# Layer 1's modulation, moved from behind layer 0's mixer to the look-ups of layer 0's expert search

## The chip, the cores and the metric

One core of a Trainium2 chip runs the whole kernel in one launch. The metric is the time of the kernel on the device in microseconds (us). Before the change it is 5706.96 us (median of 3 runs, 5706.85 to 5725.06).

## The reference

Two layers run over 512 latent tokens `x` and 256 context tokens `ctx`, 1024 wide. Everything is float32.

```
silu_c, silu_cc = silu(c), silu(c_ctx)
for l in range(2):
    mod_x = split(silu_c  @ w_mod[l] + b_mod[l], 6)      # shift, scale, gate, twice; (1024) @ (1024, 6144)
    mod_c = split(silu_cc @ w_mod[l] + b_mod[l], 6)
    h_c = layer_norm(ctx) * (1 + mod_c[1]) + mod_c[0]
    mix_c, states = token_mixer(h_c)                     # four branches; in the last layer only the states
    ctx = layer_norm(a * ctx + mod_c[2] * mix_c)
    h_c = layer_norm(ctx) * (1 + mod_c[4]) + mod_c[3]
    ctx = layer_norm(a * ctx + mod_c[5] * peer_ffn(h_c)) # not in the last layer
    # the same for x, whose scans start from the context's states
peer_ffn(h): q = h @ wq; two top-16 searches of 128 keys for each of 8 heads, top-16 of their sums,
             act = gelu(h . u[id]) * softmax(score), out = sum over 8 * 16 experts of act * v[id]
```

The modulation needs `c`, `c_ctx`, `w_mod` and `b_mod` alone. It can be made at any time before the layer that uses it.

## The kernel before

**Staging.** A layer 0 runs like this: modulation; the context's projections and scans, with x's gates and branches beside them; the context's expert search (`peer_front`); x's projections and scans (`recurrent`, in the phase "m2") with the context's expert gathers beside them; the branches' ends and the output projection (`mix_out`); x's expert search; then the experts of x. Of x's four token tiles, tile 3 gathers its experts' rows one by one; tiles 0 to 2 run through all 16384 experts densely, in chunks of 128 experts: `dense_u` (24 matmuls a chunk, of a hi and a lo part that ScalarE and VectorE split), `gates_all` (which turns the look-ups' results into gate tiles), and `dense_uv`, `dense_v`.

**The modulation.** `mod_steps(l, groups, fm)` (L466) is a generator. For each of 12 groups of 512 columns it loads 8 tiles of 256 KB through SyncE's queue, multiplies each with the 2 columns of silu(c), silu(c_ctx) into one PSUM row pair, copies the row with ScalarE, transposes it in 4 pieces, and adds the bias on VectorE into `fm` ("modfm"), with one more add for the scales. Then it yields. In float32 the profile shows two records for each of its matmuls.

**Lanes.** A helper's buffers have a prefix. In the lane "x" the weight tiles are "xwraw" and the PSUM tiles "pa" (2 banks); without a prefix they are "wraw" and "ps" (6 banks). For layer 0 there are 5 "xwraw" buffers during the mixer; in the expert search there are 3 "wraw" buffers (`WF`, L47).

**What sets the order.** The program is traced in one order. A planner then puts the instructions of each engine into a fixed order by priorities (the count of the trace), by data that is ready in its own reckoning of time, and by free buffers; each engine and SyncE's DMA queue run that order strictly. Fillers (`add`, `step`, `fill`, `drain`) are generators in lane "x" whose pieces are traced with a priority at least 200 later (`LOW`). `tick` traces pieces of the context's gathers with a priority 3000 later and not before what was traced ahead of them; it gives fixed numbers of pieces to the steps of x's scans (`RT`, `TL`). So an instruction that is traced late runs early where its engine would stand idle and its buffers are free: layer 1's modulation is traced as a filler behind `mix_out` (L1877 to L1879), but needs only silu(c) and free "xwraw" buffers, and the trace has it at 1207 to 1436 us, beside x's scans.

**The expert search.** `peer_front` (L1767) first projects the queries in 8 units (`peer_scores`), for each of which `topk_head` makes the top-16 lists of the four token tiles on VectorE; behind each of these `fill(n)` traces one dense chunk (`FD`). Then comes, for the tiles in the order 3, 0, 1, 2:

```
for i in order:
    top = self.topk(tk[i])          # the look-ups: one-hot products on VectorE
    ...                             # tile 3: gather_in, and rows for its tokens
    self.fill(m)                    # FT = 1 dense chunk
    ...                             # tiles 0 to 2: dense_in, transposes of ids and gates
```

Of the kernel before, what the change touches and what calls it, by code (L numbers as in the profile page):

```python
# [53 lines left out]
FT = 1  # L54
UO = 64
FD = 1
# [128 lines left out]
class K:  # L185
# [1578 lines left out]
                self.nc.sync.dma_start(a, acts[c])  # L1764
                self.v_chunk(l, c, a, w, acc, vv, False, c == N - 1)

    def peer_front(self, l, x, fm, s, h, order, dense=None, n=0, m=0):  # L1767


        NT = len(x)  # L1770

        self.lo_pool = True
        tk = [self.topk_tiles() for _ in range(NT)]

        def fn(u, S):
            for i in order:
                self.topk_head(u, S[i], tk[i])
                self.fill(n)
        self.peer_scores(l, h, NT, fn)
        self.lo_pool = False  # L1780
        gg, late = [], []
        for i in order:
            with self.section() as sec:
                top = self.topk(tk[i])
                if dense is not None and i < ND:

                    late.append((i, top))
                else:
                    gg.append((i, self.gather_in(l, *top)))
            self.fill(m)  # L1790
            while late and (late[0][0] != i or i == order[-1]):
                self.dense_in(*late.pop(0), *dense)
            if gg and (dense is None and len(gg) == NT or dense is not None and len(gg) == 1 and i == gg[0][0]):
                with self.section(sec):
                    rows = [self.bcast_row(fm, g, s, 1.0) for g in (3, 4)]
                    gg = [(i, (self.h_tokens(x[i], rows),) + g) for i, g in gg]
        return [g for _, g in gg]

    def run(self):
        io = self.io  # L1800
        x = [io["x"][i] for i in range(4)]
        c = [io["ctx"][i] for i in range(2)]
        y = [io["y"][i] for i in range(4)]
        fm = None
        for l in range(L):
            last = l == L - 1
            self.nw = {"": WB[l], "x": WX[l]}
            self.extra = {"": WE[0][l], "x": WE[1][l]}
            x1 = [self.d([128, 1024], f"x1_{i}", 2) for i in range(4)]
# [3 lines left out]
            with ExitStack() as mix:  # L1813
                hx = self.hx()

                mx = self.merged(512, hx)
                mix.enter_context(self.phase("mix"))
                mix.enter_context(self.sharing())
                with self.phase("m1", s1=s1, s2=s2, xs2=xs2):
                    hT = self.t([128, 2, 8, 256], "hT", 1, F32R)  # L1820
                    if fm is None:
                        fm = self.mod(0, range(4))
                    hc = self.norm_mod(c, fm, 0, 1, hT)
                    if not last:
                        self.add(self.mod_steps(l, range(4, 12), fm))
                        gates = self.add(self.gates(l, hc, 256, mc[0]))
                        self.add(self.pool_branch(l, hc, 2, 1, mc))
                        self.add(self.four_branch(l, hc, 2, 1, mc))
                    self.add(self.norm_steps(x, fm, 0, 0, hx))
                    hx = self.parts(hx)  # L1830
                    gatesx = self.add(self.gates(l, hx, 512, mx[0], range(4 if last else 2)))
                    self.add(self.pool_branch(l, hx, 4, 0, mx))
                    self.add(self.four_branch(l, hx, 4, 0, mx))
                    if not last:
                        fm1 = self.keep([128, 48, 2], "modfm", 2)
                        gatesy = self.add(self.gates(l, hx, 512, mx[0], range(2, 4)))

                    def branch(b, y, after):
                        self.add(self.scanned(l, b, hc, 2, mc, y, after), after=gates)
                    states = self.recurrent(l, hc, 2, [None] * 4, not last, FC[l], branch)  # L1840
                    states = [self.put_state(st) for st in states]
                    if not last:
                        while len(mc[2]) < 8:
                            self.fill()
                        self.mix_out(l, c, c1, fm, 1, mc[2])
                        hT = self.t([128, 2, 8, 256], "hT", 1, F32R)
                        self.lo_pool = True
                        h = self.norm_mod(c1, fm, 3, 1, hT)
                        gc = self.peer_front(l, c1, fm, 1, h, range(2), None, FC[l][6], FC[l][6])
                        accs = [self.d([128, 1024], "gacc", 4) for _ in range(2)]  # L1850
                        rows = self.gather(l, gc, accs)
                        self.ticking(rows)
                        while len(self.fillers) > 1:
                            self.fill()
                            self.tick(RE)
                    elif self.fillers[:1] != [gatesx]:
                        self.finish()
                with self.phase("m2", **(dict(s2=M2X[0], xs2=M2X[1]) if last else dict(s2=M2, s4=3, xs2=M2Y))):
                    lane = "x" if last else ""

                    def branch(b, y, after):
                        if last or b == 3:
                            self.add(self.scanned(l, b, hx, 4, mx, y, after), lane, gatesx if last else None)
                        else:
                            y = {c: self.put_state(t, "y", 4) for c, t in y.items()}
                            late.append(self.scanned(l, b, hx, 4, mx, y, after))
                    late = []
                    self.tick(RT[0])
                    self.recurrent(l, hx, 4, states, True, FX[l], branch)
                    for g in late:  # L1870
                        self.add(g, lane, gatesx)
                    while self.fillers:
                        self.fill()
                        self.tick(RT[6])
                    self.ticked()
                    hT = self.mix_out(l, x, x1, fm, 0, mx[2], self.hx)
                    if not last:  # L1877
                        self.add(self.mod_steps(l + 1, range(12), fm1))
                        self.drain()  # L1879
            if not last:  # L1880
                at = self.tc.cur_priority
                self.tc.cur_priority += GP
# [6 lines left out]
            it = [self.t((128, ND * 128), f"it{k}", 1, F16) for k in range(2)]  # L1889
            gp = self.t((128, 2, ND * 128), "gp", 1, F16)  # L1890
# [6 lines left out]
            self.extra = {"": 0, "x": 0}  # L1897
            with self.phase("fx", s2=4, s4=2, x4=2):
                self.add(gu)
                gx = self.peer_front(l, x1, fm, 0, hT, (3, 0, 1, 2), (it, gp), FD, FT)  # L1900
                self.fillers.clear()
            gen = self.gather(l, gx, [accx])
            with self.area("wk", side="right") as wk:
# [48 lines left out]
            x = x2  # L1952
            if not last:
                fm = fm1
# [119 lines left out]
```

## Time and profile before

| | us |
|---|---|
| median of the runs | 5706.96 |
| the profiled execution | 5714.13 |
| its span (core 0) | 5712.4 |
| TensorE busy | 4988.2 |
| VectorE busy | 4243.9 |
| ScalarE busy | 1949.3 |
| GpSimd busy | 1614.6 |

PE is TensorE, PEld its weight loads, DVE VectorE, ACT ScalarE, POOL GpSimd, SPq SyncE's DMA queue. Layer 0 takes the first 3300 us or so. All instructions carry line L150, a helper that records each operation; the names of the tiles tell them apart: `pa<-xwraw,sc` is a modulation matmul, `pa<-masks,xs` the transpose of its row, `ps<-hx,whi` a projection, `ps<-s,s` and `ps<-s,masks` scan work, `gat` the gathers, `oh` and `sel` the look-ups, `hx,dh` and `hx,dl` a dense chunk, `acts` its result.

### The profile page before, as it was taken

What the parts mean: (1) busy time and instruction counts of PE and PEld (TensorE: products, weight loads), DVE (VectorE), ACT (ScalarE), POOL (GpSimd) and SP (SyncE); (2) the same over time, 40 slices, a digit from 0 to 9 for tenths busy, and PEclk for the clock granted to TensorE, in tenths of its full rate; (3) what the DMA queues carried; (4) which work ended last, traced back from release to release, by engine and by line L of the source; (5) the groups of instructions that cost most, each with busy time, mean ns of one, the idle gap of its engine ahead of it and who ended that gap; (6) DMA issues with size and microseconds to landing.
All of it is one profiled execution on the core that took longest, in us unless ns stands there. A gap on an engine that the chain in (4) does not pass through costs nothing. (4 is left out here: it accounts for less than half of the span.)

```text
span 5712.4 us, 76827 instructions
## 1 busy us (share of the span) xinstructions
PE 4988.2 (87%) x26902; PEld 4198.0 (73%) x26902; DVE 4243.9 (74%) x8063; ACT 1949.3 (34%) x3711; POOL 1614.6 (28%) x1226
## 2 busy tenths in 40 slices
PE   8998878889457786699999979999888979999997
PEld 3787755763456685699987868787677969999886
DVE  3665777878778889898777786467565579977777
ACT  2444421321003332254333344233134324433333
POOL 0000344333444552444332210000002434443221
PEclk9999998989668898899999989999998989999999
DMA  6555589888878774799889863434434339988897
GB/s 214 176 167 177 166 301 321 275 277 288 276 261 296 258 236 153 256 357 343 299 306 349 317 214 125 134 103 134 129 119 135 126 109 335 363 299 314 320 332 244
DMA packets 618070, 1372.35 MB, mean 240 GB/s; under 512 B 95569, under 2 KB 229329, under 8 KB 614865
## 3 DMA queue, kind: packets, MB, share of 16 engines
q1 hardware_dynamic: 470224, 830.50, 43.0%
q0 software_dynamic: 147456, 536.94, 27.3%
q8 instruction: 211, 3.46, 0.2%
q14 instruction: 179, 1.46, 0.1%
HBM read 1225.64 MB, written 141.56 MB: 239 GB/s over the span
## 5 line engine op out<-in xcount | busy, mean ns | idle before, releaser
L150 POOL DMA_INDIRECT gat<-in_u,gidx x512 | 692.6, 1353 | 964.5 <-DVE gat L150 886.3
L150 POOL DMA_INDIRECT gat<-in_v,gidx x512 | 629.5, 1229 | 1166.3 <-DVE gacc L150 1046.7
L150 PE MATMUL ps<-hx,dh 128*128 128x384 f32 x2944 | 759.8, 339 | 0.9 <-ACT dh L150 0.9
L150 DVE SCALAR_TENSOR_TENSOR gacc<-gat,gact,gacc 128x1024 f32<-128x1024 f32 x508 | 658.7, 1297 | 96.7 <-DMA gat<-in_v,gidx 88.8
L150 DVE SCALAR_TENSOR_TENSOR gat<-gat,hb 128x1024 f32<-128x1024 f32 x512 | 618.0, 1218 | 127.1 <-DMA gat<-in_u,gidx 125.3
L150 PE MATMUL ps<-s,s 128*128 128x128 f32 (+3 forms) x2752 | 421.3, 311 | 160.3 <-issue 84.8
L150 PEld LDWEIGHTS ps<-s,s 128*128 128x128 f32 (+1 forms) x2752 | 376.7, 214 | 231.2 <-issue 119.6
L150 PEld LDWEIGHTS ps<-hx,dh 128*128 128x128 f32 x2944 | 535.4, 190 | 8.4 <-ACT dh L150 2.6
L150 PE MATMUL ps<-hx,dl 128*128 128x384 f32 x1472 | 497.6, 338 | 34.3 <-DVE dl L150 34.3
L150 ACT CAST dh<-du 128x1024 fp32r<-128x1024 f32 x256 | 269.2, 1052 | 754.4 <-PE ps L150 518.9
L150 DVE TENSOR_TENSOR vl<-dv,vh 128x1024 fp32r<-128x1024 f32 x256 | 313.3, 1224 | 200.8 <-ACT vh L150 197.4
L150 ACT CAST xwhi<-xwraw 128x512 fp32r<-128x512 f32 x352 | 217.7, 620 | 518.4 <-PE pa L150 389.7
L150 PE MATMUL ps<-hx,whi 128*128 128x512 f32 x1152 | 381.0, 399 | 8.5 <-ACT whi L150 8.4
L150 ACT CAST vh<-dv 128x1024 fp32r<-128x1024 f32 x256 | 269.2, 1052 | 341.4 <-PE ps L150 237.6
L150 PE MATMUL pa<-hx,xwhi 128*128 128x512 f32 x1152 | 376.3, 404 | 4.8 <-DVE ld L150 2.3
L150 ACT CAST whi<-wraw 128x512 fp32r<-128x512 f32 x320 | 197.9, 621 | 487.6 <-PE ps L150 272.2
L150 DVE TENSOR_TENSOR xwlo<-xwraw,xwhi 128x512 fp32r<-128x512 f32 x352 | 242.8, 692 | 159.8 <-ACT xwhi L150 149.2
L150 PE MATMUL pa<-hx,dh 128*128 128x384 f32 x1152 | 338.3, 358 | 10.5 <-ACT da L150 10.4
L150 PE MATMUL ps<-vl,gh 128*128 128x512 f32 x1024 | 318.2, 392 | 0.0
L150 PE MATMUL ps<-vh,gh 128*128 128x512 f32 x1024 | 317.4, 393 | 0.0
L150 PE MATMUL ps<-vh,gl 128*128 128x512 f32 x1024 | 317.2, 391 | 0.0
L150 PEld LDWEIGHTS ps<-hx,dl 128*128 128x128 f32 x1472 | 279.2, 190 | 36.1 <-DVE dl L150 36.0
(291 smaller groups left out, 10898.3 us busy)
## 6 DMA issues: line engine op xcount, KB each, us to landing
du<-in_ut SPq DMA_DIRECT2D x256, 512.0 KB
dv<-in_v SPq DMA_DIRECT2D x256, 512.0 KB
xwraw<-in_w_in SPq DMA_DIRECT2D x272, 256.0 KB
wraw<-in_w_in SPq DMA_DIRECT2D x176, 256.0 KB
xwraw<-in_w_mod SPq DMA_DIRECT2D x160, 256.0 KB
acts<-da SPq DMA_DIRECT2D x176, 192.0 KB
rest<-wst SPq DMA_DIRECT2D x48, 704.0 KB
W<-rest SPq DMA_DIRECT2D x22, 1536.0 KB
```

The source lines that it names most:

```text
L150: r = f(*a, **kw)
```

## The change

Layer 1's modulation is no longer a filler behind `mix_out`. `peer_front` takes a generator `beside` and advances it three steps (three of 12 column groups) behind each token tile's look-ups, so that four tiles take all 12. It now runs without a prefix: weight tiles "wraw", PSUM "ps", row "s2" of the phase "fx", at the search's own priority and not 200 later. In the last layer `beside` is empty. The context's `peer_front` is called without it.

```diff
-    def peer_front(self, l, x, fm, s, h, order, dense=None, n=0, m=0):
+    def peer_front(self, l, x, fm, s, h, order, dense=None, n=0, m=0, beside=iter(())):
...
                     gg.append((i, self.gather_in(l, *top)))
+            for _ in range(3):
+                next(beside, None)
             self.fill(m)
...
                     hT = self.mix_out(l, x, x1, fm, 0, mx[2], self.hx)
-                    if not last:
-                        self.add(self.mod_steps(l + 1, range(12), fm1))
-                        self.drain()
...
                 self.add(gu)
-                gx = self.peer_front(l, x1, fm, 0, hT, (3, 0, 1, 2), (it, gp), FD, FT)
+
+                beside = iter(()) if last else self.mod_steps(l + 1, range(12), fm1)
+                gx = self.peer_front(l, x1, fm, 0, hT, (3, 0, 1, 2), (it, gp), FD, FT, beside)
+                self.run_all(beside)
                 self.fillers.clear()
```

## Rows read from the trace of the kernel before

**Rows 1.** The page, part 1: busy us, share of the span, instructions.

```profile
PE 4988.2 (87%) x26902; PEld 4198.0 (73%) x26902; DVE 4243.9 (74%) x8063; ACT 1949.3 (34%) x3711; POOL 1614.6 (28%) x1226
```

**Rows 2.** Table of stretches of layer 0: from:to, length, busy us by engine.

```profile
core 0: us, PE busy (x) PEld busy (x) DVE busy (x) ACT busy (x) POOL busy (x), PEclk, DMA share, GB/s
1242.00:1446.00 204.00, 174.13 (x610) 75.67 (x608) 166.53 (x324) 40.57 (x69) 63.94 (x54) 0.93 0.81 278
1446.00:1720.00 274.00, 148.75 (x753) 133.18 (x752) 214.69 (x268) 24.38 (x44) 138.37 (x115) 0.66 0.82 274
1720.00:1990.00 270.00, 197.97 (x1199) 172.43 (x1198) 229.18 (x315) 97.36 (x221) 125.07 (x100) 0.87 0.81 279
1990.00:2180.00 190.00, 156.97 (x768) 139.25 (x767) 161.91 (x667) 52.25 (x92) 99.59 (x74) 0.93 0.68 227
2180.00:2312.00 132.00, 87.98 (x439) 81.22 (x439) 123.39 (x372) 37.16 (x51) 19.25 (x15) 0.83 0.40 131
2312.00:2370.00 58.00, 53.39 (x337) 51.76 (x336) 49.84 (x47) 21.17 (x47) 35.41 (x21) 0.97 0.93 326
2370.00:2430.00 60.00, 28.90 (x172) 27.78 (x170) 39.09 (x49) 10.98 (x32) 27.93 (x19) 0.72 0.81 263
2430.00:3300.00 870.00, 855.64 (x4670) 765.56 (x4669) 709.66 (x869) 349.71 (x644) 304.66 (x228) 0.99 0.92 328
```

**Rows 3.** Groups of instructions, 1242 to 1446: busy us, mean ns | idle before, releaser.

```profile
L150 PE MATMUL pa<-xwraw,sc 128*2 128x512 f32 x178 | 87.0, 612 | 7.1 <-DMA xwraw<-in_w_mod 6.9
...
L150 PE MATMUL ps<-hx,whi 128*128 128x512 f32 x80 | 25.8, 416 | 5.4 <-ACT whi L150 5.4
...
L150 PE MATMUL pa<-masks,xs 2*128 2x2 f32 x48 | 4.9, 202 | 6.2 <-ACT xs L150 6.2
```

**Rows 4.** Time line of TensorE in x's scans: start us, us, instruction.

```profile
1368.63 2.74 PE L150 MATMUL pa<-xwraw,sc 128*2 128x512 f32 x6
1371.30 1.12 PE L150 MATMUL ps<-s,masks 128*128 128x512 f32 x2
...
1375.01 1.02 PE L150 MATMUL pa<-xwraw,sc 128*2 128x512 f32 x2 [0.77 <-DMA xwraw<-in_w_mod]
...
1380.16 1.02 PE L150 MATMUL pa<-xwraw,sc 128*2 128x512 f32 x2 [0.94 <-DMA xwraw<-in_w_mod]
1382.11 1.02 PE L150 MATMUL pa<-xwraw,sc 128*2 128x512 f32 x2 [0.93 <-DMA xwraw<-in_w_mod]
```

**Rows 5.** Stretch table of the gathers' tile alone: DVE, ACT, POOL busy.

```profile
1242.00:1446.00 204.00, 64.28 (x106) 0.00 (x0) 63.94 (x54) 0.93 0.81 278
```

**Rows 6.** Time line of SyncE's queue at the end of the expert scores.

```profile
2159.01 0.33 SPq L150 DMA_DIRECT2D wraw<-in_wq  x1
2166.56 4.49 SPq L150 DMA_DIRECT2D acts<-da  x2
```

**Rows 7.** Tile "wraw", 0 to 70 us: ns min/median/max, first and last start.

```profile
L150 PE MATMUL ps<-wraw,sc x64: 590/592/1057, 9.5 to 64.5; 128*2 128x512 f32 x64
L150 SPq DMA_DIRECT2D wraw<-in_w_mod x32: 327/328/431, 4.2 to 60.4; - x32
```

**Rows 8.** Time line of TensorE: part of a dense chunk, one record left out.

```profile
2249.39 0.51 PE L150 MATMUL pa<-hx,dh 128*128 128x384 f32 x2
...
2249.91 0.51 PE L150 MATMUL pa<-hx,dh 128*128 128x384 f32 x2
```

**Rows 9.** Groups of instructions, 2180 to 2312.

```profile
L150 DVE TENSOR_TENSOR dl<-du,dh 128x1024 fp32r<-128x1024 f32 x15 | 18.3, 1217 | 0.7 <-ACT dh L150 0.7
```

**Rows 10.** Waits from 2370 to 2430: us in total, times, longest.

```profile
PE ps L150 <- DVE dl L150: 25.0, 2, 15.2
```

**Rows 11.** Time line of TensorE in the look-ups, with idle time before.

```profile
2266.51 0.45 PE L150 MATMUL ps<-masks,sel 128*128 128x128 f32 x1 [10.54 <-DVE sel L150]
...
2282.57 0.45 PE L150 MATMUL ps<-masks,sel 128*128 128x128 f32 x1 [4.10 <-DVE sel L150]
...
2290.28 0.69 PE L150 MATMUL pa<-hx,dl 128*128 128x384 f32 x1 [7.26 <-DVE dl L150]
```

## The prediction, made before the change was run

> **What bounds the kernel now.** I read the page first for shares: TensorE 87% of the span, VectorE 74%, so no engine is full over the whole kernel and the stage decides [rows 1]. Then a table of stretches around the two places of the change [rows 2]. In it the reader sees four regimes. From 1242 to 1446 us (x's scans: projections and the four state-space chunks) TensorE is busy 174.1 of 204 us and VectorE 166.5. From 1446 to 1990 both have room. From 2180 to 2312 (end of the expert scores, then the look-ups) VectorE is the bound, 123.4 of 132 us, and TensorE has 44 us free. From 2430 to 3300 TensorE is full, 855.6 of 870 us, so work that is late at 2430 is paid in full afterwards.
>
> Then the groups of the first stretch [rows 3]: 87.0 us of TensorE's 174.1 is the modulation's matmuls (178 of 192 records, two to a loaded tile), 4.9 us its row transposes; TensorE also stands idle 7.1 us for the modulation's loads and 6.2 us for its row copies. The time line [rows 4] shows why that matters: the scan's short matmuls (two of 1.12 us) stand in one in-order queue between modulation pieces of 1 to 2.7 us, and at 1375.01, 1380.16 and 1382.11 the piece at the head waits for a load while scan work stands behind it. So the modulation is no free filler there; it sits on the path that sets the end of the stretch. How much of it comes back depends on VectorE, where 64.3 us are the context's gathers [rows 5].
>
> **The change, part by part.**
>
> *Removed from x's scans.* TensorE loses 87.0 + 4.9 us of work and 7.1 + 6.2 us of waits, 105 us at most [rows 3]; the stretch could then be 99 us on TensorE alone. VectorE doesn't allow that: without the 64.3 us of gathers it has 166.5 - 64.3 = 102 us [rows 2, 5]. The gathers have a far later priority and may slide. If half of them stay, VectorE has 134 us; at 93%, the highest share that it reaches in these stretches short of the full one (123.4/132), that is 143 us, and 204 - 143 = 61 us are won. Bounds: 105 us if only TensorE held the stretch; if all gathers stay, 166.5/0.93 = 178, or 26 us; no loss, for even at 1.2 GHz throughout TensorE's other 82 us would be some 153.
>
> From that goes a clock loss. With the modulation TensorE is busy 85% and its granted clock is 0.93; in the stretch right behind it is busy 54% at 0.66, and at 73% the clock is 0.87 [rows 2]. What remains is 174 - 92 = 82 us; in 143 us that is 57%. I take 0.75: 82 x (0.93/0.75 - 1) = 20 us, half of it on the path, 10 us. Won: 51 us. The Trainium skill says in "TensorE: Matmul & The Clock Gate", section "Part 1: The HAM clock gate", that the array is throttled by default and only activity releases it, 1.2 against 2.4 GHz. The trace agrees (0.66 behind the stretch, 0.93 in it), and it is a rule against this change, since the modulation's matmuls are also what keeps the array awake beside the scans; what it would give in full is the second rival.
>
> The gathers that slide (32 us) meet 59 + 41 + 28 = 128 us of idle VectorE between 1446 and 2180 [rows 2]; I charge nothing for them. If that cover is gone they cost up to 32 us in the look-ups. The 25 MB of loads leave a stretch with a DMA share of 0.81; I give no gain for it beyond the 7.1 us already counted.
>
> *Added between the look-ups.* 96 loads of 256 KB, 192 matmul records, 48 small transposes, 12 row copies on ScalarE, 16 tiny VectorE operations. Three loads take 2.67 us of TensorE back to back (1368.63 to 1371.30 [rows 4]), 0.89 a load: 85 us, and with transposes 88 us. The loads can't start before the last expert-query weights have left their buffers: that load is issued at 2159 [rows 6], so I start at 2180. They now share three "wraw" buffers (five "xwraw" before). The row nearest to three buffers is layer 0's own start, where 32 such loads kept TensorE's queue from 9.5 to 64.5 us, 1.72 us a load [rows 7]. 96 of them: 165 us, from 2180 to 2345.
>
> In those 165 us the kernel before does 88 us at clock 0.83 plus 30 us (33/58 of 53.4) at 0.97 [rows 2], 102 us at full clock. If TensorE reaches the share it has in the search's first part, 157/190 = 0.83, it does 137 us; 88 are modulation, 49 are left, so 53 us of the dense expert chunks are pushed behind 2345. A chunk is 24 matmuls, three of them 0.52 us [rows 8], 4.2 us: 13 chunks. Their lo-part subtractions, 1.2 us each [rows 9], leave VectorE's queue in the look-ups, which frees some 15 us there.
>
> Of the 53 us a part is caught up: from 2370 to 2430 TensorE is idle 31 us [rows 2], 25 of it waiting for VectorE's chunk splits [rows 10]. With VectorE ahead by 15 us and a backlog of chunks I take 20 us back. Cost: 33 us. Bounds: below, perfect packing of 88 us into the 44 + 5 + 31 idle us leaves 8 us, and with the slow clock there even a small gain; above, all of it behind 2430, 88 us.
>
> *Waits added.* The 16 VectorE adds stand in the queue of the look-ups and wait for a transposed row; behind them the look-ups wait. ScalarE's row copies wait for a group's last matmul (beside the scans that is the 6.2 us that TensorE then waits in turn [rows 3]), and behind them stand the chunks' casts. The chunk loads and stores on SyncE share the queue with the 96 loads; two stores held it 4.5 us at 2166 [rows 6]. POOL's queue gets nothing. VectorE's own additions are on 8 columns each. What hides all this is that TensorE idles for look-up results anyway, 10.5, 4.1 and 7.3 us at a time [rows 11].
>
> *Sum.* 51 - 33 = 18 us faster. The profiled execution took 5714.1 us (5712.4 of it span), 7.2 above the median of 5707.0; taken from the median: **5689 us**.
>
> **Rivals.**
>
> *A, all hidden.* The stretch of the scans was TensorE's alone and the modulation fits into the idle time at the look-ups: 95 won, 25 lost (88 less the 165 - 102 free), 70 faster, 5637. For it: the waits for loads at the head of the queue. Against: VectorE's 166.5 us.
>
> *B, the clock takes it back.* Without the modulation the scans run at the 0.66 of the stretch behind: 82 x (0.93/0.66 - 1) = 34 us, all on the path. 61 - 34 - 33 = -6, so 5713. For it: 57% busy is near the 54% of that stretch. Against: some 26 of the 82 us are projections in one dense block [rows 3].
>
> *C, VectorE holds the scans.* All gathers stay where they are: 26 won, 33 lost, 5714. For it: the gathers are placed by ticks beside those very steps.
>
> *D, three buffers stall the search (the slower side).* Place: TensorE's in-order queue from 2180. A load that lands late holds the chunks, the index transposes and with them the first gate tiles. At 2.3 us a load the stretch ends at 2401, 56 us later; at the 30% left for chunks (49/165) 17 of these are used and 39 lost: 33 + 39 - 51 = 21 slower, 5728. It decides from 1.72 + 18/(0.7 x 96) = 2.0 us a load. For it: with five buffers the loads already came late at a DMA share of 0.81. Against: the share is 0.40 in the look-ups.
>
> *E, the change doesn't do what it says.* The order that is written out puts the modulation behind the look-ups, into the full stretch: 88 lost, 51 won, 5744. Against: it is traced before the next tile's look-up.
>
> **How the numbers follow.** A measurement here tells some 0.3% (17 us) from no change: under 5690 is faster, over 5724 slower. Chances: forecast 0.42 (own range 5665 to 5705; 0.30 of it under 5690), A 0.14, B and C 0.20 together (0.16 within, 0.04 slower), D 0.18, E 0.06. Faster 0.44, same 0.12 + 0.16 = 0.28, slower 0.04 + 0.18 + 0.06 = 0.28. The range is 5640 to 5738: it leaves out half of A's place, E, and little of D.
>
> **What would show it.** Removal: the stretch from x's first state-space projection to the first delta-rule step falls from some 204 us to 140 to 155, with no modulation in TensorE's queue, the clock at 0.7 to 0.8. Clock: under 0.7 speaks for B. VectorE: if it is over 93% busy in that stretch, C. Search: 192 records between about 2130 and 2300 (all earlier by the 51 us), 1.5 to 1.9 us a load, TensorE over 80% busy in the look-ups; waits for "wraw<-in_w_mod" over 60 us there are D. Catching up: the layer's full stretch should reach its end some 18 us before the old one. Wrong altogether if the scans don't shorten by 20 us, or if the modulation's records lie elsewhere.

## The result, and the profile after

The changed kernel is slower: 5759.5 us against 5707.5 us in the runs of the same chip, ratio 1.0077 (95% interval 1.0055 to 1.0099), some 44 us. Forecast were 18 us faster. The profiled execution took 5744.3 us, its span 5742.5, 30 more than the profiled one of before, which was itself 7 above its median.

Part 1 of the page after (columns as in [rows 1]): nearly the same work, TensorE 29 us more of it and the rest within 6 us.

```profile
PE 5017.1 (87%) x26902; PEld 4192.4 (73%) x26902; DVE 4247.9 (74%) x8063; ACT 1951.7 (34%) x3711; POOL 1610.3 (28%) x1226
```

The stretch table after, cut at the same events as [rows 2] as nearly as they are to be found (columns as there; the second and third row hold as many records of TensorE, 753 and 1199, as the same two of before):

```profile
core 0: us, PE busy (x) PEld busy (x) DVE busy (x) ACT busy (x) POOL busy (x), PEclk, DMA share, GB/s
1232.00:1429.00 197.00, 115.47 (x384) 76.04 (x384) 169.57 (x318) 33.82 (x57) 69.63 (x59) 0.70 0.58 185
1429.00:1698.00 269.00, 147.08 (x753) 131.52 (x753) 215.35 (x265) 24.45 (x44) 134.90 (x115) 0.66 0.83 279
1698.00:1967.00 269.00, 198.71 (x1199) 172.71 (x1198) 223.05 (x310) 97.52 (x221) 119.99 (x97) 0.86 0.80 271
1967.00:2150.00 183.00, 152.92 (x766) 135.91 (x764) 162.41 (x665) 52.05 (x92) 99.16 (x71) 0.94 0.71 236
2150.00:2282.00 132.00, 120.71 (x519) 79.85 (x519) 116.86 (x357) 39.21 (x55) 19.69 (x16) 0.97 0.64 208
2282.00:2400.00 118.00, 91.71 (x253) 27.95 (x253) 47.46 (x62) 10.89 (x17) 35.16 (x26) 0.90 0.80 279
2400.00:2423.00 23.00, 22.78 (x153) 22.30 (x151) 19.62 (x28) 8.91 (x21) 8.41 (x5) 1.00 0.58 173
2423.00:2670.00 247.00, 244.53 (x1883) 240.92 (x1884) 237.40 (x280) 124.82 (x372) 115.95 (x70) 0.99 1.03 361
2670.00:3330.00 660.00, 645.77 (x3053) 559.00 (x3052) 508.80 (x633) 241.53 (x322) 206.39 (x169) 0.99 0.89 319
```

Two things are to be seen. The first stretch fell from 204 to 197 us, not to 140 to 155, though TensorE's busy time fell by 59 us; VectorE's stayed (166.5, now 169.6). And behind the look-ups there is a new stretch, 2282 to 2400, in which VectorE, ScalarE and the matmul count fall away: TensorE is 92 us busy with 253 instructions, and 64 of the 92 us are modulation (115 records).

The tile "wraw" from 1900 to 2500 us (ns min/median/max, first and last start; below, why its engine sat idle before it) says when: 96 loads between 2202 and 2398, 2.04 us each.

```profile
L150 PE MATMUL ps<-wraw,sc x192: 589/592/1061, 2201.8 to 2397.1; 128*2 128x512 f32 x192
L150 SPq DMA_DIRECT2D wraw<-in_w_mod x96: 327/328/427, 2132.6 to 2393.9; - x96
...
  DMA wraw<-in_w_mod: 91.6, 85
```

The waits between 2200 and 2400 us (engine, tile, releaser: us, times, longest): TensorE and its weight loads wait 91.6 us for the modulation's weights, ScalarE 96.5 and VectorE's adds 52.2 us for TensorE.

```profile
ACT s L150 <- PE ps L150: 96.5, 13, 19.4
...
PEld ps L150 <- DMA wraw<-in_w_mod: 63.5, 58, 2.9
DVE modfm L150 <- PE ps L150: 52.2, 12, 11.3
...
PE ps L150 <- DMA wraw<-in_w_mod: 28.1, 27, 2.1
```

TensorE's time line in the look-ups shows the form of it: the dense chunks' records (tiles "hx,dh" and "hx,dl") do run between the loads, but a piece whose load is late stops them.

```profile
2215.16 0.96 PE L150 MATMUL pa<-hx,dh 128*128 128x384 f32 x4
2216.05 1.02 PE L150 MATMUL ps<-wraw,sc 128*2 128x512 f32 x2
2217.62 1.02 PE L150 MATMUL ps<-wraw,sc 128*2 128x512 f32 x2 [0.55 <-DMA wraw<-in_w_mod]
2218.57 0.44 PE L150 MATMUL pa<-hx,dl 128*128 128x384 f32 x1
```

To see where the time goes I numbered TensorE's instructions in each trace, the modulation left out, and read how much earlier (-) or later (+) the instruction that stands at a given time of before comes. The events are the same in every kernel below, the modulation's aside; some 220 of 26500 at most stand in another order (in e9 and e10 up to 800, from 1132 on). Single executions differ by up to some 10 us: the column 1200 shows it, which lies ahead of the modulation's first record in before (1207).

```
us, at before's    1200  1320  1720  2240  2640  3300
after                -3   -17   -22   -29   +32   +29
e1  no modulation    -2   -14   -18   -24   -23   -22
e2  one load         +2   -11   -14   -16   +12   +11
e3  six buffers      +9    -3    -4    -5   +36   +34
e4  one load, before -5    -7     0    -1    -5    -3
e5  e1, fewer ticks  -2   -15   -38   -41    -1     0
e6  late adds        +2   -11   -12   -16   +43   +41
e7  e2 and e6        +1   -12   -15   -16   +14   +14
e8  beside steps     -1   -14   +12   +38    +9    +7
e9  8 chunks, 4 look  -   +45    +7    +9   +24   +22
e10 12 at chunks      -   +36    -8    -2   +47   +45
e11 half at look-ups -6   -19   -23   -29   -19   -20
e12 fewer ticks      +4    +1   -16   -15   +31   +32
e13 6 and 6          +3     0    -2    +1    +1    +2
e14 9 and 3          +4    +1    -1    +6    +5    +2
```

The row of after, from its -3 at 1200: 19 us are won by 1720 and 26 by 2240, 61 are lost between 2240 and 2640, and the rest of the kernel keeps that. 14 of the 19 are won ahead of 1320, half of them ahead of 1242, and 5 behind the chunks.

### The profile page after: what moved, and what is told of

The parts are those of the page before. It is cut to its first block, busy times and chain, and to the rows that moved or that the text cites. A ratio compares the mean times of both kernels' runs of the same rounds, so it can differ in the third digit from the quotient of the medians.

```text
span 5742.5 us, 76844 instructions
## 1 busy us (share of the span) xinstructions
PE 5017.1 (87%) x26902; PEld 4192.4 (73%) x26902; DVE 4247.9 (74%) x8063; ACT 1951.7 (34%) x3711; POOL 1610.3 (28%) x1226
## 5 line engine op out<-in xcount | busy, mean ns | idle before, releaser
L150 PE MATMUL ps<-s,s 128*128 128x128 f32 (+3 forms) x2752 | 434.8, 317 | 198.7 <-DVE s L150 103.5
L150 ACT COPY s<-ps 128x512 f32<-128x512 f32 (+4 forms) x230 | 109.3, 495 | 643.1 <-PE ps L150 632.3
```

The source lines that it names most:

```text
L150: r = f(*a, **kw)
```

## The experiments

Theory at the start: the source gives little because VectorE with the gathers holds the scans, and the destination costs more than forecast because three buffers make TensorE wait. Rivals: the granted clock at the source; TensorE's room or VectorE's adds at the destination. The times of before differ a little between chips; each ratio is against the runs of its own chip.

**e1, the modulation left out** (layer 0's values stand in for layer 1's; the removal alone). Against the kernel before, cut:

```diff
-                        fm1 = self.keep([128, 48, 2], "modfm", 2)
+                        fm1 = fm
...
-                        self.add(self.mod_steps(l + 1, range(12), fm1))
-                        self.drain()
```

> Layer 1's modulation is left out (layer 1 uses layer 0's). This is the removal from x's scans alone, with nothing added in the look-ups. Theory: the scans give back some 30 us that last to the end, so 5677 us against 5707 of before; the stretch of x's scans (context gathers 184 to 238) takes 180 to 185 us as in the changed kernel, with the clock near 0.71. Rival (the gain is eaten by the context's gathers that slide into the full VectorE of the search): 5700 or more. My recorded forecast had 51 us for this step, which would be 5656.

Measured: 5699.4 against 5716.3 us, ratio 0.9971 (0.9954 to 0.9987): 17 us, little more than half of the 30 that were expected; in the traces 16 (by 1720) to 22 (by 2240), counted from 1200. This is all that any other place for the modulation could win with the rest of the kernel as it is. By the table most is won ahead of 1320. The four chunks give nothing: cut at the same events they take 126 us in before and in after and 130 here; the delta-rule steps behind them give 8 (274 and 266 us).

**e5 and e12, fewer gathers beside the chunks**: the chunk's tick of 8 gather pieces set to none, in e5 on top of e1 (so without the modulation), in e12 in the kernel before.

```diff
-RT = (20,8,2,8,21,21,9)
+RT = (20,8,2,0,21,21,9)
```

> Layer 1's modulation left out, and the 8 gather pieces that are traced behind each of x's four state-space chunks are traced later. Question: why does taking 92 us of TensorE's work out of the scans give only some 20 us? Theory VectorE: in the chunks VectorE with its gathers holds the pace (157.8 of 182 us busy without the modulation), so without these 32 gathers (39 us of VectorE) the stretch from the last state-space projection to the first delta-rule steps shortens by 20 us or more, while the whole time moves little, since the gathers come later. Rival clock: the chain runs at the 0.71 clock and the stretch stays within 8 us.

> The kernel before with its modulation beside the scans, but without the 8 gather pieces behind each of x's four state-space chunks (they are traced later). Without the modulation the same edit took 20 us out of the chunks. If the modulation in TensorE's queue and VectorE's gathers hold the chunks side by side, they now shorten by less than 8 us; if VectorE alone holds them, by some 20 us again.

Measured, one run each: e5 5718.8 against 5713.1 us, e12 5756.9 against 5714.4. At 1720 e5 stands 20 us ahead of e1. Stretch tables of the four chunks, the gathers' tile alone (DVE, ACT, POOL busy), e1 and then e5, before and then e12:

```profile
1306.00:1436.00 130.00, 55.40 (x92) 0.00 (x0) 54.90 (x46) 0.63 0.62 192
```

```profile
1305.00:1418.00 113.00, 34.98 (x58) 0.00 (x0) 33.66 (x29) 0.70 0.48 147
```

```profile
1320.00:1446.00 126.00, 52.02 (x86) 0.00 (x0) 52.42 (x43) 0.94 0.85 302
```

```profile
1321.00:1440.00 119.00, 35.05 (x58) 0.00 (x0) 36.02 (x29) 0.97 0.76 262
```

Without the modulation, 20 us of gathers less on VectorE make the chunks 17 us shorter: most of what VectorE does there is on the path. With the modulation in TensorE's queue, 17 us of gathers less make them 7 us shorter, which is e12's first answer (under 8): there the two hold the chunks side by side. So taking out the modulation alone leaves VectorE's chain in the way; whether the lower clock makes that chain longer stays open. Behind the chunks e12 catches up; from 1320 to 1720 it wins 17 us. Yet all that e5 and e12 win is gone at 2640. The gathers left for later are then waited for behind the look-ups, where VectorE's in-order queue holds the dense chunks' splits behind them. The waits from 2400 to 2580 in e12 (VectorE waited 36.2 us for gathered rows, 7.0 in before; 27.8 in e5, 5.4 in e1), and TensorE's for VectorE's splits from 2240 to 2640 (62.4 us, 28.9 in before; 66.0 in e5, 21.2 in e1):

```profile
DVE gat L150 <- DMA gat<-in_u,gidx: 36.2, 20, 5.9
```

```profile
PE ps L150 <- DVE dl L150: 62.4, 12, 12.8
```

So the gathers' amount beside the chunks is not free to choose: less of it makes the scans faster and the dense chunks slower.

**e4, the loads taken out of the kernel before**: one load for a group's eight pieces, 84 of 96 loads left out (so seven of eight pieces use the first one's weights).

```diff
             for k in range(8):
-                w = self.t([128, 512], self.pre + "wraw", self.raws())
-                nc.sync.dma_start(w, io["w_mod"][l, g, k // 2, :, k % 2])
+                if k == 0 or l == 0:
+                    w = self.t([128, 512], self.pre + "wraw", self.raws())
+                    nc.sync.dma_start(w, io["w_mod"][l, g, k // 2, :, k % 2])
```

> The kernel before, with one load for each column group of layer 1's modulation, used eight times (84 of 96 loads left out); the matmuls stay beside x's scans. If the loads' waits at the head of TensorE's queue are what the modulation costs there: 15 to 30 us faster than before, 5677 to 5692. If it is TensorE's time in the queue: within 8 us of before.

Measured: ratio 1.0004 (0.9992 to 1.0017), no difference. The late loads at the head of TensorE's queue in the scans [rows 4], on which I had built, cost nothing that shows, and neither do the 22 MB.

**e2, e6 and e7, what the destination costs.** All three change the kernel after: e2 takes out the loads by e4's edit (84 left out), e6 takes VectorE's 16 adds out of the look-ups' queue (ScalarE copies the transposed rows, and the biases are added once behind the look-ups), e7 does both. From e6, cut:

```diff
+            if l:
+                nc.scalar.copy(fm[:, 4 * g:4 * g + 4, :], pt)
+                yield
+                continue
             b = self.vec[l][:, V_BM + 4 * g:V_BM + 4 * g + 4]
...
```

> The changed kernel, but each of the 12 column groups loads one weight tile and multiplies it eight times (84 of 96 loads left out; the same 192 matmul records). Theory (three buffers starve TensorE): the modulation's span at the look-ups shrinks from 196 us to about 130, waits for in_w_mod from 92 us to under 20, and the time falls from 5744-5780 to about 5695. Rival (TensorE has no room for 88 us there, loads or not): 5735 or more. Rival (VectorE's adds hold the look-ups): waits of modfm on PE stay near 50 us and the look-ups end as late.

> The changed kernel, with ScalarE copying the transposed rows and one VectorE add of the biases (and two for the scales) behind all look-ups, so that no look-up stands behind an add that waits for TensorE. Theory VectorE's adds (52 us of waits in 2200 to 2400): the look-ups and the index transposes end earlier and the time falls by 20 us or more against the changed kernel. Rival (TensorE's queue and the loads set it): within 10 us of the changed kernel, 5735 to 5770, because the index transposes stand behind the modulation in TensorE's queue anyway.

> Both: one load a column group (84 of 96 loads left out) and the adds behind the look-ups. What is left of the cost is TensorE's own time. If TensorE's room is the limit: 5715 to 5730, as with one load alone (5728). If adds and loads are two separate stalls: 5705 or less.

Measured: e2 1.0022 (1.0008 to 1.0037), e6 1.0074 (1.0049 to 1.0099), e7 1.0032 (1.0019 to 1.0046). The adds cost nothing that shows (e6 is as slow as after). Without the loads' waits half of the loss goes, and half stays: e2's 5728 us lies between its theory (5695) and the rival that TensorE has no room (5735 or more). In e2 TensorE no longer waits for these weights, and its 96 pieces still take 146 us, 1.52 us each, for the chunks' matmuls run between them:

```profile
L150 PE MATMUL ps<-wraw,sc x192: 591/592/593, 2213.9 to 2359.5; 128*2 128x512 f32 x192
```

What the half that stays is, the same stretch (between the marks 2240 and 2640 of before) shows in e1, e11 (below), e7 and after, in this order:

```profile
2216.00:2617.00 401.00, 330.07 (x2308) 319.34 (x2308) 365.16 (x460) 160.26 (x425) 169.94 (x104) 0.91 0.84 290
```

```profile
2210.00:2621.00 411.00, 375.38 (x2429) 317.69 (x2429) 366.92 (x468) 163.16 (x431) 172.20 (x104) 0.96 0.91 313
```

```profile
2224.00:2654.00 430.00, 422.61 (x2547) 324.25 (x2546) 366.31 (x463) 165.48 (x447) 166.84 (x104) 0.99 0.80 277
```

```profile
2211.00:2672.00 461.00, 427.73 (x2552) 323.62 (x2551) 368.16 (x476) 166.27 (x437) 164.84 (x104) 0.97 0.89 307
```

The first number behind the length is TensorE's busy time. Without modulation it has 401 - 330 = 71 us free. The modulation adds 422.6 - 330.1 = 92.5. In e7 TensorE is full (422.6 of 430): 92.5 less the 63.5 that are used is 29 us, TensorE's room alone. After takes 31 us more for the same work (e2, where only the loads are taken out, shows the same step, 28 us from 2240 to 2640 against 61): that is the waiting for loads, with whatever the 84 loads cost the other transfers.

**e3, six buffers instead of three** in layer 0's search.

```diff
-            self.extra = {"": 0, "x": 0}
+            self.extra = {"": 0 if last else 3, "x": 0}
```

> The changed kernel with six instead of three wraw buffers in x's expert search of layer 0; all loads are made. Theory (latency of a load over three buffers sets 2.04 us a load): six buffers bring it to 1.2 us or less, the modulation ends some 60 us earlier, time 5695 to 5715. Rival (DMA bandwidth: 0.80 share in that stretch): a load still takes 1.7 us or more, time 5735 or more.

Measured: 5746.7 us, ratio 1.0051 (1.0034 to 1.0068). The tile's lines as above:

```profile
L150 PE MATMUL ps<-wraw,sc x192: 591/592/1061, 2222.7 to 2384.5; 128*2 128x512 f32 x192
...
  DMA wraw<-in_w_mod: 62.1, 56
```

1.69 us a load instead of 2.04, and still 62 us of waits. The theory (1.2 us or less, 5695 to 5715) failed, and the rival's numbers came; that the DMA's bandwidth is the reason, as it says, is not shown. In its trace the part from 2240 to 2640 grows by 41 us, in after's by 61; but this execution was 12 us behind after's already at 1200, and the ratio's interval overlaps with that of after. By the trace more buffers give back part of the waits, not the room.

**e11, half of the groups between the look-ups**, two per look-up of the first three token tiles; the other six are left out (layer 0's values stand in).

```diff
-            for _ in range(3):
+            for _ in range(2):
                 next(beside, None)
...
-                beside = iter(()) if last else self.mod_steps(l + 1, range(12), fm1)
+                beside = iter(()) if last else self.mod_steps(l + 1, range(6), fm1)
...
```

> The changed kernel with six of the 12 column groups, two behind each of the first three look-ups (the other six are left out and layer 0's values stand in for them). Theory (TensorE's room of some 72 us between 2240 and 2640): half the work fits, the cost over no modulation at all is under 12 us instead of 54, the time 5690 to 5705. Rival (a cost for each load and each group, from stalls of the in-order queues): half of 54, 5720 or more.

Measured: 5707.6 us, ratio 0.9994 (0.9982 to 1.0006), 13 us above e1's ratio; in the trace the stretch is 10 us longer than e1's (411 against 401) for 45 us of added work. Half of the groups cost a sixth (by the traces) to a fifth (by the times) of what all cost: the cost is far from proportional to the work, and TensorE's idle time is the place to look for the reason.

**e8, e9 and e10, other places in x's scans**, with all the work done: each group tied to a step of the program, ahead of which it is traced, instead of taken as a filler. e8: the eight delta-rule steps; e10: the four chunks, three each; e9: the chunks, two each, and one in each look-up. From e10, cut:

```diff
...
+            if self.late is not None and NT == 4:
+                at = self.tc.cur_priority
+                self.tc.cur_priority += LOW
+                with self.lane("x"), self.section(secs[-2] or loc):
+                    for _ in range(3):
+                        next(self.late, None)
+                self.tc.cur_priority = at
             self.fill(F[1])
             self.tick(RT[3])
...
```

> The kernel before, with layer 1's modulation tied to x's eight delta-rule steps (12 column groups, two and one by turns, each not before its step), in lane x with five buffers. There TensorE is 54% busy at a clock of 0.66. Theory: the removal's 20 us stay and the matmuls raise the clock of the steps, 5690 to 5705 against 5707 to 5716 of before. Rival (the loads wait at the head of TensorE's queue at a DMA share of 0.82, and the steps are one chain): 5730 or more.

> The kernel before, with eight of layer 1's column groups tied to x's four state-space chunks (two each, lane x, five buffers) and the other four between the look-ups (one a token tile, three buffers). The runs so far say that the projections ahead of the chunks gain 12 to 14 us when they have no modulation in TensorE's queue, and that the look-ups have some 72 us of TensorE's time free for 29 us of work. Theory (room): 5695 to 5705, 5 to 15 us under before. Rival (a load that lands late holds the in-order queue wherever it stands): 5715 or more.

> The kernel before, with all 12 column groups tied to x's four state-space chunks, three each, none in the projections ahead of them and none in the look-ups. VectorE with its gathers holds the chunks (126 us without and 126 us with 56 us of modulation), so 88 us of TensorE's work may hide there: theory 5700 to 5710, at or a little under before. Rival (88 us do not fit and spill into the delta-rule steps, where they cost as in the run with the steps): 5720 or more.

Measured: e8 1.0017 (1.0008 to 1.0027), e9 1.0052 (1.0035 to 1.0069), e10 1.0097 (1.0080 to 1.0114): all slower, and all three theories failed (e8's 5726 us stays under its rival's 5730 as well). e10 has no modulation in the look-ups and stands at -2 us at 2240; it loses 49 us behind them. Its waits from 2400 to 2580 name the same line as e12's:

```profile
DVE gat L150 <- DMA gat<-in_u,gidx: 40.8, 21, 4.7
```

From 1000 to 2312 us VectorE's gathers sum to 488 us in before, 470 in e12 and 464 in e10; the waits for gathered rows from 2312 to 2640 to 18, 36 and 41. So an order that hands the gathers less of VectorE ahead of the look-ups pays behind them, also where no modulation is there; that rests on e5 and e12, which change nothing else, and e10 fits it. Why the groups tied to the chunks push the gathers back in e10 I did not follow further. e8 is 38 us late at 2240 and only 9 at 2640: its gathers are ahead (500 us by 2312, 1 us of waits).

**e13 and e14, the work split**, all of it done: six groups beside the scans as before and six between the look-ups (two each in three), and nine and three. Open was whether half of the work costs as little with the other half done too. From e13, cut:

```diff
+                    if not last:
+                        self.add(self.mod_steps(l + 1, range(6), fm1))
+                        self.drain()
...
-            for _ in range(3):
+            for _ in range(2):
...
+                beside = iter(()) if last else self.mod_steps(l + 1, range(6, 12), fm1)
```

> The whole modulation is done: six groups beside x's scans as before, six between the look-ups, two per look-up of the first three token tiles. Theory (the two terms are not linear: TensorE has room for about six groups between the look-ups, at some 8 us, and x's scans give back only what stands ahead of the chunks): the scans give back what the first kernel's last six groups held, 0 to 10 us, the look-ups cost 0 to 8: ratio 0.996 to 1.002. Rival (both terms linear: half of 20 won, half of 54 lost): 17 us slower, ratio 1.003. Rival (VectorE and the gathers set both): the gathers that slide out of the chunks are waited for behind the look-ups, and the ratio is 1.003 or more with waits of VectorE for gathered rows over 30 us between 2400 and 2580 us.

> The whole modulation is done: nine groups beside x's scans as before, three between the look-ups, one per look-up of the first three token tiles. Theory (room for six groups between the look-ups): the three cost nothing there, and the scans give back 0 to 6 us: ratio 0.998 to 1.001. Rival (linear): a quarter of 20 won, a quarter of 54 lost, 8 us slower, ratio 1.0015. Rival (gathers): waits of VectorE for gathered rows over 30 us between 2400 and 2580 us, ratio 1.003 or more.

Measured: e13 1.0001 (0.9991 to 1.0010), e14 0.9998 (0.9989 to 1.0007). The linear rival's 1.003 for e13 is outside the interval: the six groups cost next to nothing, as e11 said; both theories' ranges hold. VectorE's waits for gathered rows from 2400 to 2580 are 4.3 and 6.6 us, so the gathers' rival falls too. But nothing is won either: with six groups left beside the scans these are as late as before (-2 us at 1720). No version that does all the work beats the kernel before.

## Why the prediction was wrong

**The step that failed first: "Removed from x's scans", 51 us won.** The stretch that the step is about fell by 7 us (204 to 197). With the 7 that came ahead of it, where the modulation had begun at 1207, and the 5 behind it, 19 us were won by 1720; e1's time says 17. The step let half of the gathers slide and took VectorE to be 93% busy. None slid: VectorE's gathers in the stretch are 70.3 us after, 64.3 before [rows 5]. And VectorE is 86% busy (169.6 of 197 us). The two parts of the stretch (columns as in the table; projections, then chunks), before and then after, show what held:

```profile
1242.00:1320.00 78.00, 66.88 (x219) 31.89 (x217) 65.35 (x146) 20.90 (x34) 11.52 (x11) 0.91 0.76 239
1320.00:1446.00 126.00, 107.25 (x392) 43.78 (x392) 101.17 (x179) 19.66 (x35) 52.42 (x43) 0.94 0.85 302
```

```profile
1232.00:1303.00 71.00, 42.51 (x139) 29.88 (x140) 67.14 (x145) 18.73 (x30) 14.41 (x13) 0.75 0.50 161
1303.00:1429.00 126.00, 72.96 (x246) 46.16 (x245) 102.43 (x174) 15.09 (x27) 55.22 (x46) 0.66 0.63 198
```

In the projections VectorE is now 67.1 of 71 us busy, 95%, and little more was to be had. The chunks are as long as before; VectorE is 81% busy in them, and 17 us of their length hang on the 20 us of its gathers that e5 took away; of the other 35 no run tells. That is rival C, though its 26 us were more than came; its sign, VectorE over 93% busy, showed in the projections only. The sign that I had called "wrong altogether", scans that do not shorten by 20 us, was met. My reading that pieces with late loads at the head of the queue hold the scans was refuted by e4. It was a time line read as a cause: each wait is there, but without it the stretch ends no earlier.

**The clock** fell to 0.70 (0.75 taken). Rival B asks for less than 0.7: the chunks alone stand at 0.66, the whole stretch does not. TensorE's other work took 115 us where it had taken 82, 33 us more, which is the size that B gave it; how much of that lies on the path is not shown. e5 shortened the chunks by 17 us at 0.70, so the clock did not set their length by itself. No run kept it high with the modulation gone; its share of the missing 30 us stays open.

**The second: "Added between the look-ups", 33 us lost.** Measured 60 (461 against 401 us). The time at which it ends was off by two terms. Start: I took 2180, with what the scans gave some 2151, because the loads could start; the first piece ran at 2202, though its load was issued at 2133. Price: 2.04 us a load, against 1.72 from layer 0's start [rows 7]. That row was no price of a load alone: beside its 32 loads 25 of the other lane were issued, at a DMA share of 0.82; and in the search the chunks' matmuls stand between the pieces, 1.52 us apart even in e2. With both terms it ends at 2398 where 2345 less the gain was forecast. What made the cost is the idle time that the work could use. The forecast used 55 us of it (137 - 102 = 35 beside the loads, 20 by catching up) for 88 us of work. In after TensorE has 98 us more to do than in e1 (427.7 - 330.1) and uses 38 of its 71 us; 33 stay idle, 28.1 of them ahead of late loads. In e7, without these waits, 63.5 are used for 92.5 us of work, and the cost is 29: the room was judged about right, and the waits for loads, 31 us, are the term that was too small. Filled to the last microsecond the place costs some 22. The lower bound of 8 took all 80 idle us between 2180 and 2430 as usable; the upper bound of 88 holds.

**Rival D** is what happened at the destination: waits for the loads of 91.6 us (over 60 was its sign), 2.04 us a load (it decides from 2.0). That the end at 2398 is near its 2401 is luck, for that was 2.3 us a load from 2180 on. With the smaller gain at the source its 5728 became 5744 to 5759. The sign of the forecast fell on both terms: with 51 won even the true loss would have made it 9 slower, and with the true gain of 16 to 26 even the loss that I forecast would have.

**Right**: what is late at 2430 is paid in full (+32 at 2640, +29 at 3300); VectorE's adds cost nothing that shows (e6); E fell, since the modulation ran among the look-ups.

## What to carry to other kernels

An engine's work that leaves a stretch is worth at most what the other engines in the chain allow: before counting it, look at which small operations of the other engines (here gathers that were meant as fillers) stand in the path, and price the removal by a run that leaves the work out. Idle time at a destination can be spent once: compare the added work with the sum of the idle time up to where the engine is full, and move no more than that. Filler that is delayed on one engine can come back as waits where its data is needed (e5, e12).

## What the runs showed of the hardware

The spacing of 256 KB loads through few buffers was no constant, and no price of a load: with three buffers it was 1.72 us at the start of the kernel [rows 7] at a DMA share of 0.82, and 2.04 us in the search (0.64 to 0.80), where TensorE had the chunks to do between the pieces; six buffers gave 1.69, and with 84 of the 96 loads left out (e2) the pieces still stood 1.52 us apart.

The granted clock in x's scans fell from 0.93 to 0.70 when the filler matmuls left them. The Trainium skill's "TensorE: Matmul & The Clock Gate", section "Part 1: The HAM clock gate", says that activity releases the clock. The trace agrees in this. The four chunks took 126 us at 0.94 with the modulation and 126 us at 0.66 without it; what the clock alone is worth there no run shows.
